# A delta-rule stage rewoven: one inversion on GpSimd, q projected ahead of z, weight loads from ScalarE's queue

## The chip, the cores and the metric

The kernel runs on one core of a Trainium2 chip. A core has five engines with queues of their own: TensorE (matrix products, called PE in the profile, with its weight loads as PEld), VectorE (DVE), ScalarE (ACT), GpSimd (POOL) and SyncE (SP), which here only orders transfers. The metric is the time on the device, in microseconds.

## The reference

Three token mixers and four feed-forward networks stand one after another on 256 tokens (272 with 16 meta tokens in the first part) of 1024 features, batch 1, in float32:

```python
h = concat(meta, x)
h = h + 0.5 * rmsnorm(swiglu(rmsnorm(h)))            # d_ff 2816
h = h + rmsnorm(mlstm_mixer(rmsnorm(h)))
h = h + 0.5 * rmsnorm(swiglu(rmsnorm(h)))
h = h[:, 16:]
h = h + gated_deltanet(rmsnorm(h))                   # the stage that is changed
h = h + conv_gated_mlp(rmsnorm(h))                   # its evictions carry the bias transfers
h = h + sliding_window_sink_attention(rmsnorm(h))    # uses a relative bias table
h = h + conv_gated_mlp(rmsnorm(h))
return rmsnorm(h)
```

The gated delta rule projects h to q and k (8 heads of 128), v and z (16 heads of 128) and two gates, runs a causal convolution of width 4 and a silu over q, k and v, normalizes q and k, and then, for each v head, with cumulated gates gc:

```python
decay = tril(exp(gc[:, None] - gc[None, :]))
m     = strict_tril((beta * k) @ k.T * decay)
t_mat = inverse(m + eye)                  # unit lower triangle
...                                       # u = t_mat @ (beta v), w = t_mat @ (beta k exp(gc))
o     = q_dec @ state + (q @ k.T * decay) @ v_new
o     = rmsnorm(o) * silu(z)
out   = o @ w_out
```

## The kernel before

Activations lie transposed in SBUF, features on partitions, tokens along the free axis. Weights come from HBM in halves of eight 128x128 tiles (512 KB, `load_half`): SyncE orders the transfer into one of four buffers `raw`, ScalarE casts it in two pieces to a high part `whi`, and VectorE subtracts to get the low part `wlo`. Each weight tile is then used in three matmuls (`mm3`, L250 to L252): high x high, high x low, low x high. `wtile` asks for halves three ahead, and five pairs of high and low parts are kept. One output block of 128 rows over 1024 inputs is 8 tiles, 24 matmuls, one half of weights.

The delta-rule stage is written in the order that a small planner, `Weave`, gives. It has fillers (the projections of the blocks in `GD_ORDER`, then the output projection `op_all`) and chains of dependent steps. A chain's step yields its cost on TensorE, a latency and its cost on VectorE; the planner advances a clock by them, takes a chain's step when its time has come, and otherwise one weight tile of the filler. The costs (`pe=0.32, dve=0.14` for one tile, `INVERT_COST = 55.0`) are figures in the source; they set the order in which instructions are written, and the engines then wait for each other by semaphores. The compiler keeps the order of each engine's queue near to it.

The chains: `norms` and `gates2` make the gate sums gc; they go to DRAM (`gcd`) and come back as 16 rows spread over all partitions (`gload`). `stage1(q8)`, for each key head, makes k k^T and q k^T, the decays from those rows on ScalarE, and the products U, N21 and A on VectorE; U goes to DRAM (`ud`). `front(0)` runs `stage1` of heads 0 to 3, `front(1)` of 4 to 7. `invert(hf)` loads the 64 diagonal blocks of 32x32 of one half into `B` (one block on each partition), and inverts them on GpSimd in 31 steps of two instructions (L1006 and L1011) on 64 partitions, copies (L1012) and stores to `xyd`. `levels(q8)` loads a head's U and its inverted blocks (`XY`, four transfers), joins the blocks to 128x128 in two levels with small matmuls (L1046 to L1076), and goes on with `solve` and `outp`, which ends with the parts that the output projection reads. `op_all` takes a head's parts as soon as its mark "h" stands. So `levels(0)` to `levels(3)` wait for `invert(0)` and `levels(4)` to `levels(7)` for `invert(1)`.

`outp` normalizes with `rsqrt_dve`, 14 small VectorE instructions, and scales with four ScalarE instructions from PSUM. `tanh_silu` and `zp` use tanh on ScalarE.

In the feed-forward network behind, `background` holds small jobs that are run one at every second eviction; among them eight transfers of 256 KB on GpSimd's queue that spread the bias table (`bias_tile`, L1215), each followed by an empty job.

Of the kernel before, what the change touches and what calls it, by code (L numbers as in the profile page):

```python
# [22 lines left out]
SEQ = 256  # L23
# [15 lines left out]
INVERT_COST = 55.0  # L39
GD_ORDER = [(kind, m) for kind, a, b in (("k", 0, 8), ("q", 0, 4), ("z", 0, 8), ("q", 4, 8), ("z", 8, 16), ("v", 0, 16))  # L40
# [80 lines left out]
def stack_kernel(ctx, tc, w, xt, cols, rows, gw, baw, rel, kc, kb, out):  # L121
# [31 lines left out]
    whole = {}  # L153

# [3 lines left out]
    def load_half(u, raw=None):  # L158
        if raw is None:
            raw = whole.get(u)  # L160
            if raw is None:
                raw = wraw.tile([128, 1024], F32, name="raw", tag="raw")
            lastw[0] = nc.sync.dma_start(out=raw, in_=w[u // 2, :, (u % 2) * 1024:(u % 2) * 1024 + 1024])
# [8 lines left out]
        for c in ((0, 512), (512, 1024)) if u == 0 else ((0, 1024),):  # L172
            V.tensor_tensor(out=lo[:, c[0]:c[1]], in0=raw[:, c[0]:c[1]], in1=hi[:, c[0]:c[1]].bitcast(F32),  # L173
                            op=ALU.subtract)
# [520 lines left out]
    ud = [gdr.tile([16, UG], F32, name=f"ud{i}") for i in range(2)]  # L695
    gcd = gdr.tile([16, 256], F32, name="gcd")
    xyd = [gdr.tile([64, 32, 64], F32, name=f"xyd{i}") for i in range(2)]
# [19 lines left out]
    with tc.tile_pool(name="gd", bufs=1) as gp, tc.tile_pool(name="gw", bufs=2) as gq:  # L717
        def unit():
            return gp.tile([128, SEQ], F32, name="u1k", tag="u1k", bufs=55)

        def unit_r():
            return gp.tile([128, SEQ], F32R, name="u1k", tag="u1k", bufs=55)
# [21 lines left out]
        fill = Weave(pe=0.32, dve=0.14)  # L744
# [15 lines left out]
        def ev_qk(m, ps):  # L760
            y = conv4((m + 8) % 16, ps, m >= 4)
            dst = unit()
            (kT if m < 8 else qT)[m % 8] = dst
            tanh_silu(dst, y)
            t = fill.work(1.2 if m >= 4 else 1.55)
            fill.free.append(t)
            fill.later(sumsq(m, dst), fill.work(0.34, t + 0.6 - fill.now) + 0.3)
# [21 lines left out]
        def vp(m):  # L789
# [9 lines left out]
            t = fill.work(1.2)  # L799
            fill.free.append(t)  # L800
            fill.later(vt(m, y), fill.work(0.34, t + 0.6 - fill.now) + 0.3)
# [71 lines left out]
        gct = gp.tile([16, SEQ], F32, name="gct")  # L873
        gcb = {}

        def gload(vh):
            if vh < 16:
                gcb[vh] = unit()
                nc.sync.dma_start(out=gcb[vh], in_=bass.AP(tensor=gcd.tensor, offset=gcd.offset + 256 * vh,
                                                           ap=[[0, 128], [1, 256]]))  # L880

        def gates2():
# [18 lines left out]
            yield 0.0, 1.5, 3.6  # L901
# [7 lines left out]
            pgt = ps_ax()  # L909
            for i in range(2):  # L910
                T_.transpose(pgt[:16, i * 128:i * 128 + 128], gc[:, i, :], ident)
            S.copy(gct, pgt[:16, 0:256])
            nc.sync.dma_start(out=gcd, in_=gct)
            yield 0.43, 2.5, 0.0
            gload(0)
            gload(1)
            gload(2)
            yield 0.0, 2.5, 0.0
# [4 lines left out]
        def urows(g):  # L923
            t = ud[g // 16]
            return bass.AP(tensor=t.tensor, offset=t.offset + (g % 16) * UG, ap=[[128, 128], [UG, 2], [1, 128]])

        def zp(m):
# [11 lines left out]
            fill.free.append(fill.work(0.34, 0.7))  # L939
            fill.mark("z", m)  # L940

        def stage1(q8):
# [10 lines left out]
            U, A[q8], N21[q8] = [unit(), unit()], [unit(), unit(), unit()], unit()  # L953
            for j in range(2):
                vh = 2 * q8 + j
                pg = gcb.pop(vh)
# [16 lines left out]
                V.tensor_tensor(out=A[q8][j].rearrange("p (a b) -> p a b", a=2), in0=pqm, in1=dv, op=ALU.mult)  # L973
                gload(vh + 3)
                fill.work(1.9)
                yield 0.64, 0.3, 0.0

        def front(hf):
            for q8 in range(4 * hf, 4 * hf + 4):
                while ("q", 8 + q8) not in fill.done:  # L980
                    yield 0.0, 0.5, 0.0
                yield from stage1(q8)
            fill.mark("s", hf)
# [7 lines left out]
        lastinv = [None]  # L991
        xyt = [gp.tile([128, 4, 256], F32, name=f"XY{i}") for i in range(3)]
        for t in xyt:
            P_.memset(t, 0.0)

        def invert(hf):
            p0 = 64 * hf
            pr = slice(p0, p0 + 64)
            X, Y = Z[pr, :, :, 0], Z[pr, :, :, 1]
            nc.sync.dma_start(out=B[pr], in_=bass.AP(tensor=ud[hf].tensor, offset=ud[hf].offset,  # L1000
                                                     ap=[[129 * 32, 64], [128, 32], [1, 32]]))
            first = None
            for i in range(31):
                n = 31 - i
                t = tmp[pr, 0:n * (i + 1)].rearrange("p (r j) -> p r j", r=n)
                ins = P_.tensor_tensor(out=t, in0=X[:, i, 0:i + 1].unsqueeze(1).to_broadcast([64, n, i + 1]),  # L1006
                                 in1=B[pr, i, i + 1:32].unsqueeze(2).to_broadcast([64, n, i + 1]), op=ALU.mult)
                if first is None and lastinv[0] is not None:
                    after(lastinv[0], ins)
                first = ins  # L1010
                P_.tensor_tensor(out=X[:, i + 1:32, 0:i + 1], in0=X[:, i + 1:32, 0:i + 1], in1=t, op=ALU.add)  # L1011
            lastinv[0] = P_.tensor_copy(Y, X.rearrange("p i j -> p j i"))  # L1012
            nc.gpsimd.dma_start(out=xyd[hf], in_=Z[pr].rearrange("p a b t -> p a (b t)"))
            fill.pool = max(fill.pool, fill.dve + 3.0) + INVERT_COST
            yield 0.0, fill.pool + 4.0 - fill.now, 0.0
            fill.mark("i", hf)

        def levels(q8):
# [3 lines left out]
            if q8 < 6:  # L1022
                XY = xyt[q8 % 3]
            elif q8 == 6:
                XY = gp.tile([128, 4, 256], F32, name="XY", tag="B")
                P_.memset(XY, 0.0)
            else:
                XY = gp.tile([128, 2048], F32, name="XY", tag="Z")[:, 0:1024].rearrange("p (g c) -> p g c", g=4)
                P_.memset(XY, 0.0)
            src = xyd[q8 // 4]  # L1030
            for a in range(4):
                ins = nc.sync.dma_start(out=XY[32 * a:32 * a + 32, :, 64 * a:64 * a + 64], in_=bass.AP(
                    tensor=src.tensor, offset=src.offset + (16 * (q8 % 4) + a) * 2048,
                    ap=[[64, 32], [4 * 2048, 4], [1, 64]]))
                after(lastw[0], ins)
            xyv = XY.rearrange("p g (c t) -> p g c t", t=2)
            X, Y = xyv[:, :, :, 0], xyv[:, :, :, 1]
            yield 0.0, 3.0, 0.0
# [5 lines left out]
            for b in (0, 64):  # L1044
                for g in range(4):
                    ins = T_.matmul(pr[b + 32:b + 64, g * 32:g * 32 + 32], us(g, b, 32, b + 32, 32), X[b:b + 32, g, b:b + 32],  # L1046
                                    start=True, stop=True)
                    if b == 0 and g == 0:
                        after(lastmm[0], ins)
# [15 lines left out]
            yield 1.0, 0.4, 0.8  # L1065
# [11 lines left out]
            yield 0.43, 0.4, 0.3  # L1077
            yield from solve(q8, Y)

        def solve(q8, Y):  # L1080
# [18 lines left out]
            yield 0.43, 0.4, 0.34  # L1099
            pw3 = ps_mm("mm")  # L1100
            for j in range(2):
# [3 lines left out]
                             scale=cc[:, 1, vh:vh + 1])  # L1105
            yield 0.43, 1.0, 0.0
            yield from outp(q8, pc)

        def outp(q8, pc):
# [15 lines left out]
            V.scalar_tensor_tensor(out=rv.rearrange("p (j i) -> p j i", j=2),  # L1125
# [330 lines left out]
```

## Time and profile before

| what | value |
|---|---|
| median of 3 runs | 1335.73 us (1334.15, 1335.73, 1347.11) |
| profiled execution | 1347.61 us |
| its span, first to last instruction | 1345.2 us |
| mean granted TensorE clock | 0.974 |
| TensorE busy | 97% of the span |
| VectorE, ScalarE, GpSimd busy | 70%, 59%, 8% |
| HBM read | 209.09 MB, 159 GB/s over the span |

The span is that of the instructions; the execution's own time has 2.4 us around it. A busy TensorE is one that has a matmul in its pipeline, whatever its clock; the granted clock is the share of full speed, 1.0 being 2.4 GHz and 0.5 being 1.2 GHz. The delta-rule stage runs from about 550 to 865 us of the span.

### The profile page before, as it was taken

Reading aid. Unit: us, or ns where it says so; the run is one execution under the profiler, and the core shown is the slowest. Engines: PE = TensorE matmul, PEld = TensorE weight load, DVE = VectorE, ACT = ScalarE, POOL = GpSimd, SP = SyncE. Lnnn points to the kernel's source line nnn. Section 1 sums busy time; section 2 is a strip of 40 time slices with the busy share of each in tenths; the row PEclk is TensorE's granted clock in tenths of the full one; section 3 lists DMA queues with packets and bytes.
Section 4 is the critical chain, followed back from the end, with each engine's and each line's share of the span. In section 5 each row is a group of like instructions: output and inputs, shape, how many; then the busy total and the mean of one; then the engine's idle time right before and its main releaser. Section 6 shows DMA issues by size and latency. Waiting matters only on the chain.

```text
span 1345.2 us, 27310 instructions
## 1 busy us (share of the span) xinstructions
PE 1304.8 (97%) x10635; PEld 1263.6 (94%) x10635; DVE 937.2 (70%) x1858; ACT 787.5 (59%) x1822; POOL 107.8 (8%) x163
## 2 busy tenths in 40 slices
PE   8999999999999999999898999999899999999997
PEld 8999999987999999999897899999899989999997
DVE  7866546775687764487894756887896686898852
ACT  6544445654665554466653746766665576777640
POOL 0000000000000000100598300001000000000000
PEclk9999999998999999999896998999999999999999
DMA  7755543541375555226554352468766432476540
GB/s 255 243 176 176 173 157 127 158 142 47 111 246 184 186 186 172 82 96 191 166 174 134 106 158 80 157 165 210 219 195 228 158 111 72 150 235 196 186 168 32
DMA packets 77761, 215.47 MB, mean 160 GB/s; under 512 B 16245, under 2 KB 27045, under 8 KB 77504
## 3 DMA queue, kind: packets, MB, share of 16 engines
q1 hardware_dynamic: 76224, 209.36, 48.8%
q0 software_dynamic: 1120, 3.85, 1.8%
q8 instruction: 84, 1.38, 0.4%
q10 hardware_dynamic: 288, 0.52, 0.1%
q14 instruction: 45, 0.37, 0.1%
HBM read 209.09 MB, written 4.60 MB: 159 GB/s over the span
## 4 chain that ended last, share of the span: by engine, by line
PE 78%; DMA 5%; DVE 5%; POOL 4%; ACT 4%; issue 2%; SPq 0%; DVEq 0%; ACTq 0%; POOLq 0%
PE mm L250 12%; PE mm L252 12%; PE mm L251 12%; PE st L250 7%; PE st L251 7%; PE st L252 7%; DMA raw<-in_w 4%; POOL tmp L1006 2%; PE mm L268 2%; POOL Z L1011 2%; PE mm L270 2%; PE mm L272 2%; DVE wlo L173 1%; ACT whi L171 1%; PE st L268 1%
## 5 line engine op out<-in xcount | busy, mean ns | idle before, releaser
L171 ACT CAST whi<-raw 128x512 fp32r<-128x512 f32 x752 | 438.1, 616 | 342.8 <-PE mm L251 118.9
L173 DVE TENSOR_TENSOR wlo<-raw,whi 128x1024 fp32r<-128x1024 f32 (+1 forms) x377 | 461.7, 1226 | 153.0 <-ACT whi L171 145.3
L252 PE MATMUL mm<-xh,wlo 128*128 128x256 f32 (+1 forms) x1040 | 295.4, 284 | 2.7 <-DVE wlo L173 2.7
L250 PE MATMUL mm<-xh,whi 128*128 128x256 f32 (+1 forms) x1040 | 295.7, 285 | 1.9 <-DVE fu L439 1.9
L251 PE MATMUL mm<-xl,whi 128*128 128x256 f32 (+1 forms) x1040 | 294.9, 284 | 0.0
L250 PE MATMUL st<-xh,whi 128*128 128x256 f32 (+1 forms) x720 | 208.3, 289 | 1.9 <-DVE fu L439 1.9
L251 PE MATMUL st<-xl,whi 128*128 128x256 f32 (+1 forms) x720 | 206.9, 287 | 0.0
L252 PE MATMUL st<-xh,wlo 128*128 128x256 f32 (+1 forms) x720 | 206.5, 287 | 0.1
L252 PEld LDWEIGHTS mm<-xh,wlo 128*128 128x128 f32 x1040 | 196.7, 189 | 3.2 <-DVE wlo L173 3.1
L250 PEld LDWEIGHTS mm<-xh,whi 128*128 128x128 f32 x1040 | 196.7, 189 | 2.3 <-ACT fu L436 2.1
L251 PEld LDWEIGHTS mm<-xl,whi 128*128 128x128 f32 x1040 | 196.4, 189 | 0.7 <-DVE xl L380 0.6
L250 PEld LDWEIGHTS st<-xh,whi 128*128 128x128 f32 x720 | 138.6, 192 | 3.2 <-ACT whi L171 2.0
L252 PEld LDWEIGHTS st<-xh,wlo 128*128 128x128 f32 x720 | 138.4, 192 | 0.4 <-DVE wlo L173 0.3
L251 PEld LDWEIGHTS st<-xl,whi 128*128 128x128 f32 x720 | 138.4, 192 | 0.1
L250 PE MATMUL mm<-hh,whi 128*128 128x256 f32 (+1 forms) x352 | 99.6, 283 | 0.0
L251 PE MATMUL mm<-hl,whi 128*128 128x256 f32 (+1 forms) x352 | 99.6, 283 | 0.0
L252 PE MATMUL mm<-hh,wlo 128*128 128x256 f32 (+1 forms) x352 | 99.6, 283 | 0.0
L250 PEld LDWEIGHTS mm<-hh,whi 128*128 128x128 f32 x352 | 67.0, 190 | 0.0
L251 PEld LDWEIGHTS mm<-hl,whi 128*128 128x128 f32 x352 | 66.5, 189 | 0.0
L252 PEld LDWEIGHTS mm<-hh,wlo 128*128 128x128 f32 x352 | 66.5, 189 | 0.0
L439 DVE SCALAR_TENSOR_TENSOR fu<-mm,colt,fu 128x255 f32<-128x255 f32 x108 | 51.2, 478 | 12.6 <-ACT fu L436 12.5
L1006 POOL TENSOR_TENSOR tmp<-Z,B 64x31 f32<-64x31 f32 (+15 forms) x62 | 43.9, 709 | 91.8 <-DMA B<-ud 87.1
(488 smaller groups left out, 2697.2 us busy)
## 6 DMA issues: line engine op xcount, KB each, us to landing
raw<-in_w SPq DMA_DIRECT2D x377, 512.0 KB, 4.0
u1k<-gcd SPq DMA_DIRECT2D x16, 128.0 KB, 3.5
ud<-u1k SPq DMA_DIRECT2D x16, 128.0 KB, 2.9
u1k<-ud SPq DMA_DIRECT2D x16, 128.0 KB, 2.5
Tb<-bvd POOLq DMA_DIRECT2D x8, 256.0 KB, 7.6
gx<-in_w SPq DMA_DIRECT2D x2, 512.0 KB, 6.9
xyd<-Z POOLq DMA_DIRECT2D x2, 512.0 KB, 5.2
XY<-xyd SPq DMA_DIRECT2D x32, 32.0 KB, 1.9
```

The costliest lines, as they stand in the source:

```text
L171: S.copy(hi[:, c[0]:c[1]], raw[:, c[0]:c[1]])
L173: V.tensor_tensor(out=lo[:, c[0]:c[1]], in0=raw[:, c[0]:c[1]], in1=hi[:, c[0]:c[1]].bitcast(F32), op=ALU.subtract)
L250: T_.matmul(ps, hi, xhh, start=first, stop=False)
L251: T_.matmul(ps, hi, xll, start=False, stop=False)
L252: lastmm[0] = T_.matmul(ps, lo, xhh, start=False, stop=last)
L268: T_.matmul(pss[j], wts[j][0], xhh, start=(k == 0), stop=False)
L270: T_.matmul(pss[j], wts[j][1], xhh, start=False, stop=False)
L272: T_.matmul(pss[j], wts[j][0], xll, start=False, stop=(k == kt - 1))
L439: V.scalar_tensor_tensor(out=t[:, d:], in0=ps[:, :T - d], scalar=wc(2 - d), in1=t[:, d:], op0=ALU.mult, op1=ALU.add)
L1006: ins = P_.tensor_tensor(out=t, in0=X[:, i, 0:i + 1].unsqueeze(1).to_broadcast([64, n, i + 1]), in1=B[pr, i, i + 1:32].unsqueeze(2).to_bro ...
L1011: P_.tensor_tensor(out=X[:, i + 1:32, 0:i + 1], in0=X[:, i + 1:32, 0:i + 1], in1=t, op=ALU.add)
```

## The change

The two halves of `front` and `invert` become one: `stage1` of all eight heads in a row, then one inversion on 128 partitions, and all `levels` wait for it; `levels(3)` and later also wait for `solve` of three heads earlier (mark "y"), and `XY` takes three tiles in turn, two of which lie where `Z` was. `B` is loaded in two transfers, one after each four heads. In `GD_ORDER` all of q comes before z. The gate sums no longer go through DRAM: TensorE transposes a broadcast column into PSUM for each head (`pgs`), and ScalarE reads that. While the fillers run, weight transfers are ordered on ScalarE's queue (`wq`), and outside of the planned time of the inversion every second half's low part is made on GpSimd (`share`); one of the products A moves to GpSimd too. In `outp` roots on ScalarE and a reciprocal replace `rsqrt_dve`, and two VectorE products replace the four scalings. The planner's costs change, and `fill.sp` spaces the loads of `levels`. The 8 bias transfers become 16 of half the size, one for every job.

```diff
-INVERT_COST = 55.0
-GD_ORDER = [... (("k", 0, 8), ("q", 0, 4), ("z", 0, 8), ("q", 4, 8), ("z", 8, 16), ("v", 0, 16))
+INVERT_COST = 54.0
+GD_ORDER = [... (("k", 0, 8), ("q", 0, 8), ("z", 0, 16), ("v", 0, 16))
...
+    wq, share = [nc.sync], [False]
-            lastw[0] = nc.sync.dma_start(out=raw, in_=w[...])
+            lastw[0] = wq[0].dma_start(out=raw, in_=w[...])
-            V.tensor_tensor(out=lo[...], in0=raw[...], in1=hi[...], op=ALU.subtract)
+            (P_ if share[0] and u % 2 else V).tensor_tensor(out=lo[...], in0=raw[...], in1=hi[...], op=ALU.subtract)
...
-        fill = Weave(pe=0.32, dve=0.14)
+        fill = Weave(pe=0.355, dve=0.08)
...
-            pgt = ps_ax()                      # gates2: gc to DRAM and back
-            S.copy(gct, pgt[:16, 0:256])
-            nc.sync.dma_start(out=gcd, in_=gct)
-            gload(0); gload(1); gload(2)
...
+            pgs = ps_mm("mm")                  # stage1
             for j in range(2):
-                pg = gcb.pop(vh)
+                pg = pgs[:, j * 256:j * 256 + 256]
+                for i in range(2):
+                    T_.transpose(pg[:, i * 128:i * 128 + 128], gc[:, i, vh:vh + 1].to_broadcast([128, 128]), ident)
...
-                V.tensor_tensor(out=A[q8][j]..., in0=pqm, in1=dv, op=ALU.mult)
-                gload(vh + 3)
-                fill.work(1.9)
-                yield 0.64, 0.3, 0.0
+                P_.tensor_tensor(out=A[q8][j]..., in0=pqm, in1=dv, op=ALU.mult)
+                t = fill.work(1.46)
+                yield 0.86, max(0.3, t - fill.now - 2.4), 0.0
...
-        def front(hf):
-            for q8 in range(4 * hf, 4 * hf + 4):
+        def front():
+            for q8 in range(8):
                 ...
+                if q8 % 4 == 3:
+                    pr = slice(16 * q8 - 48, 16 * q8 + 16)
+                    nc.sync.dma_start(out=B[pr], in_=bass.AP(tensor=ud.tensor, ...))
...
+        def invert():
+            share[0] = False
+            fill.fill_dve = 0.16
             for i in range(31):
-                ins = P_.tensor_tensor(out=t, in0=X[...].to_broadcast([64, n, i + 1]), ...)
+                P_.tensor_tensor(out=t, in0=X[...].to_broadcast([128, n, i + 1]), ...)
                 P_.tensor_tensor(out=X[...], in0=X[...], in1=t, op=ALU.add)
+            P_.tensor_copy(Y, X.rearrange("p i j -> p j i"))
+            for hf in range(2):
+                nc.gpsimd.dma_start(out=xyd[pr], in_=Z[pr]...)
+            fill.pool = max(fill.now, fill.dve) + 9.0 + INVERT_COST
+            yield 0.0, fill.pool + 3.0 - fill.now, 0.0
+            share[0] = True
...
-            ro = rsqrt_dve(rv, 4, sm)          # outp
-            for g in range(4):
-                S.activation(out=ob[g], in_=po[...], func=AF.Copy, scale=ro[:, g:g + 1])
+            for i in range(2):
+                S.activation(out=rvv[:, :, i], in_=ssv[:, :, i], func=AF.Sqrt, scale=4.0 / 128.0,
+                             bias=nq2[:, i, q8:q8 + 1])
+            V.reciprocal(rv, rv)
+            for j in range(2):
+                V.tensor_tensor(out=obs[j]..., in0=po[...], in1=rv[...].to_broadcast([128, 2, 128]), op=ALU.mult)
...
+        wq[0], share[0] = nc.scalar, True
-                       ([("g",)], front(0)), ([("s", 0)], invert(0)), ([("s", 0)], front(1)),
-                       ([("s", 1), ("i", 0)], invert(1))]
+                       ([("g",)], front()), ([("s",)], invert())]
         for q8 in range(8):
-            cond = [("i", q8 // 4)]
-            if 3 <= q8 < 6:
-                cond.append(("h", q8 - 3))
+            cond = [("i",)]
+            if q8 >= 3:
+                cond.append(("y", q8 - 3))
...
-    for a in range(8):
-        background += [lambda a=a: bias_tile(a), lambda: None]
+    for a in range(16):
+        background += [lambda a=a: bias_tile(a)]
```

## Rows read from the trace of the kernel before

**Rows 1.** The page, part 1: TensorE's busy time, share, instructions.
```profile
PE 1304.8 (97%) x10635; PEld 1263.6 (94%) x10635; DVE 937.2 (70%) x1858; ACT 787.5 (59%) x1822; POOL 107.8 (8%) x163
```

**Rows 2.** Windows: length, busy time and instructions by engine, granted clock, DMA share, GB/s.
```profile
450.00:500.00 50.00, 50.00 (x426) 50.00 (x425) 32.73 (x46) 25.15 (x50) 0.00 (x0) 1.00 0.59 186
...
575.00:865.00 290.00, 272.79 (x2332) 259.29 (x2331) 207.75 (x542) 175.81 (x496) 94.70 (x133) 0.91 0.45 138
...
625.00:655.00 30.00, 24.05 (x158) 23.18 (x157) 22.34 (x61) 22.21 (x62) 4.17 (x9) 0.83 0.67 192
...
715.00:755.00 40.00, 34.65 (x286) 31.36 (x286) 19.19 (x53) 18.37 (x59) 33.86 (x49) 0.66 0.46 143
755.00:795.00 40.00, 38.60 (x344) 36.43 (x345) 31.98 (x91) 29.14 (x90) 0.95 (x1) 1.00 0.39 113
795.00:825.00 30.00, 30.00 (x341) 27.15 (x340) 10.43 (x25) 11.42 (x37) 0.00 (x0) 0.77 0.36 121
...
885.00:905.00 20.00, 17.34 (x145) 16.93 (x144) 16.22 (x30) 11.40 (x25) 1.28 (x3) 1.00 0.72 179
...
940.00:960.00 20.00, 16.24 (x136) 15.89 (x136) 15.62 (x27) 11.74 (x26) 0.18 (x1) 1.00 0.86 230
```

**Rows 3.** Timeline of SyncE's queue, 685 to 760 us: start, length, what.
```profile
693.20 0.94 SPq L1021 DMA_DIRECT2D u1k<-ud  x2
710.24 1.76 SPq L1032 DMA_DIRECT2D XY<-xyd  x4
...
717.95 22.92 SPq L163 DMA_DIRECT2D raw<-in_w  x7
```

**Rows 4.** Timeline of ScalarE, 710 to 735 us.
```profile
722.03 1.14 ACT L171 CAST whi<-raw 128x512 fp32r<-128x512 f32 x2 [8.94 <-DMA raw<-in_w]
```

**Rows 5.** The chain of waits, 600 to 870 us: start, length, what.
```profile
616.61 2.48 DMA gcd<-gct
619.11 6.61 DMA u1k<-gcd
...
643.18 3.13 DMA ud<-u1k
646.47 3.60 DMA B<-ud
651.61 1.39 POOL tmp L1006
...
702.52 2.03 POOL Z L1012
```

**Rows 6.** Source line L1363, output transfers on ScalarE's queue: shortest, median, longest ns.
```profile
L1363 ACTq DMA_DIRECT2D out_t<-o x2: 338/357/376, 1340.4 to 1342.0; - x2
```

**Rows 7.** Timeline of all engines, 700 to 760 us, VectorE and GpSimd side by side.
```profile
700.75 1.30 DVE L173 TENSOR_TENSOR wlo<-raw,whi 128x1024 fp32r<-128x1024 f32 x1
...
701.04 1.09 POOL L1006 TENSOR_TENSOR tmp<-Z,B 64x31 f32<-64x31 f32 x1
...
702.22 0.24 POOL L1011 TENSOR_TENSOR Z<-Z,tmp 64x31 f32<-64x31 f32 x1
...
702.52 2.02 POOL L1012 COPY Z<-Z 64x1024 f32<-64x1024 f32 x1
...
703.22 1.61 DVE L758 SCALAR_TENSOR_TENSOR gy<-vs,gy 128x256 f32<-128x256 f32 x1
```

**Rows 8.** Timeline of GpSimd, 677 to 694 us.
```profile
685.69 0.69 POOL L1011 TENSOR_TENSOR Z<-Z,tmp 64x231 f32<-64x231 f32 x1
```

**Rows 9.** Groups by line, 560 to 900 us: busy us, mean ns; idle before.
```profile
L1131 ACT ACTIVATE u1k<-mm,rq_y 128x128 f32<-128x128 f32 x32 | 9.2, 376 | 2.1 <-DVE rq_y L292 2.1
...
L290 DVE TENSOR_TENSOR rq_t<-rq_t,rq_y 128x4 f32<-128x4 f32 (+1 forms) x27 | 4.3, 162 | 0.4
```

**Rows 10.** The page, part 6, DMA issues: KB each, median us to landing.
```profile
Tb<-bvd POOLq DMA_DIRECT2D x8, 256.0 KB, 7.6
```

**Rows 11.** Tile `raw`, 880 to 960 us: its transfers, shortest, median, longest.
```profile
DMA to landing us min/median/max: 3.5/5.9/9.3
```

More of the change, by code (lines that the diff above doesn't have):

```diff
@@ L694, in stack_kernel @@
     UG = 4 * 129 * 32
-    ud = [gdr.tile([16, UG], F32, name=f"ud{i}") for i in range(2)]
-    gcd = gdr.tile([16, 256], F32, name="gcd")
-    xyd = [gdr.tile([64, 32, 64], F32, name=f"xyd{i}") for i in range(2)]
+    ud = gdr.tile([32, UG], F32, name="ud")
+    xyd = gdr.tile([128, 32, 64], F32, name="xyd")
     n3 = []
@@ L764, in ev_qk @@
             tanh_silu(dst, y)
-            t = fill.work(1.2 if m >= 4 else 1.55)
+            t = fill.work(1.43 if m >= 4 else 1.85)
             fill.free.append(t)
-            fill.later(sumsq(m, dst), fill.work(0.34, t + 0.6 - fill.now) + 0.3)
+            fill.later(sumsq(m, dst), fill.work(0.47, t + 0.6 - fill.now) + 0.3)
         def sumsq(m, src):
@@ L798, in vp @@
             tanh_silu(y, y)
-            t = fill.work(1.2)
+            t = fill.work(1.43)
             fill.free.append(t)
-            fill.later(vt(m, y), fill.work(0.34, t + 0.6 - fill.now) + 0.3)
+            fill.later(vt(m, y), fill.work(0.47, t + 0.6 - fill.now) + 0.3)
         def vt(m, y):
@@ L989, in stack_kernel @@
         tmp = gp.tile([128, 256], F32, name="tmp")
[L991 to L1002, printed above, removed]
+        xyt = []
@@ L1018, in levels @@
+            yield 0.0, fill.pool + 3.0 - fill.now, 0.0
+            fill.mark("i")
+            share[0] = True
+            fill.fill_dve = 0.08
+            fill.sp = fill.now
         def levels(q8):
@@ L1021, in levels @@
                 nc.sync.dma_start(out=u[j], in_=urows(4 * q8 + 2 * j))
[L1022 to L1030, printed above, removed]
+            XY = xyt[q8 % 3]
             for a in range(4):
-                ins = nc.sync.dma_start(out=XY[32 * a:32 * a + 32, :, 64 * a:64 * a + 64], in_=bass.AP(
-                    tensor=src.tensor, offset=src.offset + (16 * (q8 % 4) + a) * 2048,
+                nc.sync.dma_start(out=XY[32 * a:32 * a + 32, :, 64 * a:64 * a + 64], in_=bass.AP(
+                    tensor=xyd.tensor, offset=xyd.offset + (16 * q8 + a) * 2048,
                     ap=[[64, 32], [4 * 2048, 4], [1, 64]]))
-                after(lastw[0], ins)
+            fill.sp = max(fill.sp, fill.now) + 2.8
             xyv = XY.rearrange("p g (c t) -> p g c t", t=2)
             X, Y = xyv[:, :, :, 0], xyv[:, :, :, 1]
-            yield 0.0, 3.0, 0.0
+            yield 0.0, fill.sp + 2.0 - fill.now, 0.0
             def us(g, r0, nr, c0, ncl):
@@ L1045, in levels @@
                 for g in range(4):
[L1046 to L1049, printed above, removed]
+                    T_.matmul(pr[b + 32:b + 64, g * 32:g * 32 + 32], us(g, b, 32, b + 32, 32), X[b:b + 32, g, b:b + 32],
+                              start=True, stop=True)
             for b in (32, 96):
```

89 lines of the change are left out of this document (39 added, 50 removed).

## The prediction

> **What bounds the kernel now.** I began with the page: TensorE is busy 97% of the span [rows 1], so a gain can only come from stretches in which it idles or is clocked down. The view of windows finds them: 50 us of plain feed-forward hold 426 matmuls, 0.117 us each, so a filler block of 24 weight matmuls takes 2.8 us; in a stretch the loss is its length less busy time times granted clock [rows 2]. The delta-rule stage (575 to 865 us) loses 290 - 272.8 x 0.91, about 40 us; its parts: 10.0 us at 625 to 655 (first half of `stage1`; 30 - 24.05 x 0.83), 17.1 at 715 to 755 (40 - 34.65 x 0.66) and 6.9 at 795 to 825 [rows 2]. The feed-forward part behind it loses 2.7 us at 885 to 905 and 3.8 at 940 to 960, where the bias transfers run [rows 2]. These 46 us are all the change can win; the rest of the page is TensorE at its pace.
>
> The SyncE timeline explains the largest loss: after the weight loads that end at 693.20 come two `u1k<-ud` loads of `levels(0)` and then four `XY<-xyd`, which start only at 710.24, when the first inversion has stored its result; the next weight load stands behind them and goes at 717.95 [rows 3]. So no weights were ordered for 25 us. ScalarE's next cast starts at 722.03 after 8.94 us of waiting for `raw` [rows 4], TensorE runs dry, and its granted clock is 0.66 in that stretch [rows 2], that is, part of it at 1.2 instead of 2.4 GHz, after an idle stretch.
>
> The chain of waits gives the second: the cumulated gates go through DRAM, 2.48 + 6.61 us [rows 5], then four key heads of `stage1` take from 625.7 to 643.2, then 3.13 us store and 3.60 us load, then GpSimd inverts from 651.6 to 702.5 [rows 5], and the second half of the heads starts after that. So `levels(4)` to `levels(7)` have their data some 40 us after the first four.
>
> **The change, part by part.** *Weight loads on ScalarE's queue.* They no longer stand behind `XY<-xyd`, and the 25 us hole goes. Each issue costs ScalarE 0.357 us, as the output's two there do [rows 6]; about 60 in the stage are 21 us, and ScalarE is busy 175.8 of 290 us [rows 2], so they fit into its idle time and cost the path nothing while the queue doesn't wait. What is new: a load waits for its `raw` buffer, that is, for the low part of four halves earlier, and behind it on ScalarE stand casts, PSUM copies and `stage1`'s exponentials. At no wait the cost is 0; at 1 us for each load it is 60 us of ScalarE. I take 1 us of path in all, since a load is needed only when four halves (11 us) are used up.
>
> A sentence of the Trainium skill speaks against this part: by "Trainium Kernel Development and Optimization", section Key Constraints, transfers issued from several engines' queues share the same DMA engines, and this saves only the issue time. The trace disagrees here, for the queue's order cost 25 us [rows 3] and issue time is a third of a microsecond [rows 6]; by that sentence the part would win next to nothing, which is the second rival below.
>
> *One inversion on 128 partitions, q ahead of z, gates transposed on TensorE.* Gone are the 9.1 us through DRAM [rows 5]. `stage1` of all eight heads runs in one go: at the rate of rows 5 (17.5 us for four) 35 us, from about 616 to 651; with 6.7 us store and load, inversion from 658. Its 62 steps on 128 partitions I take at the same 51 us as 64 partitions took [rows 5]; the bounds are that and twice that, since no row has such a step on 128 partitions. So `xyd` is written at 709 and all eight heads' data are there at about 716 instead of four at 710 and four at 757. Until then TensorE has the 32 blocks of z and v, 90 us, plus 14 us of `stage1` by the planner's 0.86 a head: 104 for the 100 us from 616. The cover just suffices, with 4 us over, some 10 with what is lost on the way. Then three heads' chains run (a chain is 5.7 us of TensorE by the planner's own figures, 17 for three) while the output projection waits for the first of them, some 25 to 30 us: about 12 us lost, partly at the lower clock, as at 795 to 825 now [rows 2]. So 17.1 + 6.9 becomes 12 to 13: **11 us won** (bounds 0 and 20).
>
> *stage1 itself.* Now the planner spaces its steps by VectorE's backlog and no gate load is awaited: of 10.0 us [rows 2] I leave 2.5. The added 32 transposes at 0.117 us each (the matmul pace of rows 2) are 3.8. **4 us won** (bounds -3 and 7). A third tile of the four `mm` banks for each head can hold up the next head's products; that is in the lower bound.
>
> *Half the low parts on GpSimd.* VectorE took 1.30 us for one [rows 7]. GpSimd's add of 231 elements took 0.69 us [rows 8] and of 31 elements 0.24 [rows 7]; the slope, 2.25 ns an element, gives about 2.5 us for 1024 (my value; bounds 1.3 as VectorE and 5). About 20 of them relieve VectorE of 26 us. But the two engines exclude each other: a 31-element product on GpSimd lasted 1.09 us beside a low part on VectorE, and VectorE's `gy<-vs,gy` lasted 1.61 us beside GpSimd's copy [rows 7]. So of the 26 us about half comes back as waits. None of it is on TensorE's path unless a low part is later than the 11 us for which its halves are cast ahead: 0 (bounds -4 and 3).
>
> The Trainium skill's "SBUF — State Buffer", section Who interferes with whom, says that a VectorE instruction with two inputs in SBUF and a GpSimd instruction that reads SBUF fully block each other; the trace agrees (1.61 us for 256 elements, where the low part takes 1.30 for 1024 [rows 7]). By that rule every GpSimd low part can hold up each such VectorE instruction for up to its 2.5 us, and the relief would be nil, which my zero already allows.
>
> *Roots on ScalarE in `outp`.* Away go 14 VectorE steps of 0.16 us, the four scalings on ScalarE at 0.376 us [rows 9]; in come two roots, a reciprocal and two VectorE products. Some 2 us less in each chain, and only the last counts at the end: **1 us** (bounds -3, if table loads between tanh and root fall among the v blocks, and 3).
>
> *Bias in 16 transfers.* The 256 KB transfers take 7.6 us to land [rows 10], and beside them weight loads take a median of 5.9 and up to 9.3 us, against 3.5 at best [rows 11]. Halved and spread one a step, the burst is half as long: of 6.5 us **3 won** (bounds 0 and 6.5).
>
> **Sum.** 11 + 4 + 1 + 3 - 1 = 18 us of the profiled execution, 1347.6 us (its span is 1345.2). The three timed runs have a median of 1335.7; the profiled one and one other stand 12 us higher. What lies in these 12 us no row says; if it is the lowered clock, the median has less to win. 34.65 x 0.34 is 11.8 us in 715 to 755 alone [rows 2]. So 10 to 18 us come off the median; I take 17, since the dry queue is in every run: **1319 us**.
>
> **Rivals.** *Nearly everything goes (1300).* Chains and fillers overlap as now at 755 to 795, where 40 us lose 1.4 [rows 2], and the lost 46 us shrink to 10. For it: the planner's figure for three matmuls becomes 0.355, which fits 3 x 0.117 [rows 2]. Against: the cover after 716 is thin.
>
> *The hole only moves (1331).* ScalarE's queue, in order, now holds casts behind loads that wait for low parts, or its exponentials and casts fill it in `stage1`; the 11 us shrink to 1 or 2, and 1335.7 - 5 remains. For it: ScalarE is already busy 22.2 of 30 us at 625 to 655 and gets a load more per block [rows 2].
>
> *The inversion comes too late (1360), slower.* There is one inversion and no head's chain before it; if a step on 128 partitions takes up to twice as long, or waits for VectorE's two-input instructions, data come at up to 767 instead of 716. TensorE then has about 10 us of blocks in reserve and stands still for the rest: 1335.7 - 17 + 51 - 10 = 1360. It decides from 27 us of lateness on (17 won and 10 in reserve); low parts queued behind the steps on GpSimd would add to it. For it: a step of 31 elements lasted 1.09 us beside a low part, where one alone took 0.24 [rows 7]. Against: the same happened in the 51 us that I use.
>
> The Trainium skill's "GPSIMD Engine Reference", section 2 (Architecture), says that each of eight cores serves its own 16 partitions and all get every instruction; by that 128 partitions take no longer than 64. No run here shows it yet; it speaks against this rival.
>
> **How the numbers follow.** Forecast 0.49, nearly everything 0.11, the hole moves 0.24, too late 0.16 (whole or half). A difference of 1% is 13 us, about the spread of the three runs, and what can be told from no change. The forecast's own width (10 to 20 us off) puts a tenth of it within 1%; so faster by over 1%: 0.44 + 0.11 = 0.55. Within 1%: 0.05 + 0.22 = 0.27. Slower by over 1%: 0.16 and 0.02 of the moved hole, 0.18. The range reaches from the better rival, 1299, to a lateness of 37 us, 1345; outside stay a part of the first and the doubled inversion.
>
> **What would show it.** After: no gap of over 10 us between weight loads; one inversion of about 51 us from about 658; all L1046-like matmuls after 716 and in threes; in 625 to 655 a clock of 1.0; a loss of some 12 us behind 716; raw loads under 7 us beside the bias. Wrong if casts wait for loads held on ScalarE, if GpSimd's steps are longer on 128 partitions, or if the v blocks end before 710.

## The result and the profile after

The changed kernel takes **1360.59 us** (median, 1355.42 to 1363.15), the kernel before 1335.74 in the same comparison: ratio **1.0156**, 95% interval 1.012 to 1.0193 (the two medians alone give 1.0186; the four times of the kernel before go from 1334.15 to 1347.11). It is slower by 1.6%, not faster by 1.2%. The profiled execution has a span of 1361.4 us and a time of 1363.15.

Page of the changed kernel, part 1 (answers [rows 1]), and the bias transfers of part 6 (KB each, median us to landing; [rows 10]):

```profile
PE 1298.9 (95%) x10665; PEld 1259.9 (93%) x10665; DVE 914.1 (67%) x1727; ACT 780.0 (57%) x1805; POOL 129.0 (9%) x149
...
Tb<-bvd POOLq DMA_DIRECT2D x16, 128.0 KB, 5.9
```

TensorE idles for 1361.4 - 1298.9 = 62.5 us, before for 1345.2 - 1304.8 = 40.4 [rows 1]. The windows of the changed kernel say where (columns as in [rows 2]):

```profile
585.00:685.00 100.00, 96.11 (x752) 93.13 (x752) 69.31 (x189) 61.01 (x162) 41.32 (x40) 0.97 0.50 152
625.00:655.00 30.00, 29.44 (x230) 28.24 (x229) 16.27 (x53) 20.45 (x60) 15.17 (x13) 1.00 0.55 154
685.00:825.00 140.00, 101.45 (x942) 95.15 (x941) 69.80 (x131) 63.63 (x181) 47.49 (x57) 0.79 0.36 110
705.00:735.00 30.00, 1.26 (x11) 1.05 (x9) 0.36 (x1) 0.54 (x3) 19.53 (x34) 0.56 0.20 44
905.00:1000.00 95.00, 95.00 (x811) 94.98 (x810) 81.65 (x140) 64.24 (x137) 13.90 (x28) 1.00 0.79 211
```

For 30 us from 705, TensorE, VectorE and ScalarE all do next to nothing; only GpSimd works. By the prediction's measure (length less busy time times granted clock) 685 to 825 loses 140 - 101.45 x 0.79 = 59.9 us. The same stretch of the kernel before, which holds the 17.1 and 6.9 us of [rows 2]:

```profile
585.00:685.00 100.00, 93.28 (x725) 91.07 (x725) 83.06 (x217) 64.52 (x168) 31.66 (x41) 0.95 0.56 170
685.00:825.00 140.00, 130.51 (x1203) 120.96 (x1202) 85.78 (x207) 76.57 (x227) 61.49 (x90) 0.85 0.43 130
825.00:905.00 80.00, 76.34 (x635) 73.92 (x634) 67.81 (x175) 58.70 (x151) 3.42 (x7) 1.00 0.48 139
905.00:1000.00 95.00, 91.09 (x767) 90.53 (x766) 76.85 (x128) 60.69 (x129) 4.61 (x13) 1.00 0.74 214
```

That is 29.1 us lost before, so 31 us came in, while `stage1` (585 to 685) loses 6.8 instead of 11.4 and the stretch beside the bias 0 instead of 3.9. (How far such losses differ between two executions of the same instructions is shown at d_bias16: by some 5 us in 685 to 825.)

Who stopped first? The view of waits of the changed kernel, 695 to 745 us (us in all, times, longest):

```profile
ACT Vn L810 <- DMA XZ<-xyd: 31.9, 1, 31.9
DVE gy L758 <- ACT vs L757: 30.1, 1, 30.1
...
PE ax L808 <- DVE gy L758: 29.6, 1, 29.6
```

Read from below: TensorE waits for VectorE, VectorE for ScalarE, ScalarE for a load of `XZ`. But line 810, a copy of a v head, reads no `XZ`. The timeline of ScalarE shows what stands ahead of it (answers [rows 4]; ACTq rows are its DMA issues):

```profile
702.09 0.47 ACT L737 ACTIVATE gy<-st,colt 128x256 f32<-128x256 f32 x1
734.08 0.34 ACTq L164 DMA_DIRECT2D raw<-in_w  x1
734.46 0.37 ACT L810 ACTIVATE Vn<-ax,nkh 128x128 f32<-128x128 f32 x1 [31.90 <-DMA XZ<-xyd]
```

What stands ahead of the copy is a weight load. SyncE's timeline in the same time (answers [rows 3]):

```profile
672.93 11.50 SPq L1009 DMA_DIRECT2D u1k<-ud  x6
728.24 2.91 SPq L1012 DMA_DIRECT2D XYB<-xyd  x4
731.97 3.63 SPq L1012 DMA_DIRECT2D XZ<-xyd  x8
```

SyncE waits for the inverse until 728.24, as before until 710.24. The weight loads have left its queue, and still one of them goes out only at 734.08. The order of the compiled program, with the semaphores each instruction waits for, tells why. It is the program's listing and no view of the profile (`[waits ...]`; the first number counts an engine's instructions):

```
SyncE    204 L1012 DMA XYB<-xyd [waits DMAHW5,DMASW3,Pool]
         205 to 207 XYB<-xyd    [waits DMAHW6] [DMAHW7] [DMAHW0]
         208 L1012 DMA XZ<-xyd  [waits DMAHW2,DMASW4,Pool]
         209 L1012 DMA XZ<-xyd  [waits DMAHW3]
         210 to 215 XZ<-xyd     [waits DMAHW5] [6] [7,Pool] [0] [1] [2]
ScalarE  873 L164 DMA raw<-in_w [waits DMAHW1]   (its cast: waits DMAHW1)
         876 L164 DMA raw<-in_w                  (its cast: waits DMAHW4)
         887 L737 ACTIVATE gy<-st,colt
         888 L164 DMA raw<-in_w [waits DMAHW3]   (its cast: waits DMAHW3)
         889 L810 ACTIVATE Vn<-ax,nkh
```

The transfers of the two queues take turns at eight completion semaphores, 0 to 7, in the order of the program: XYB has 5, 6, 7, 0, a weight load 1, XZ 2 and 3, a weight load 4, XZ 5, 6, 7, 0, 1, 2, and then the weight load at place 888 is again at 3. Before it may use 3, the second XZ transfer, on the other queue, must have landed. That one belongs to the row at 731.97, the second of its eight issues; the chain of waits has it at 732.32 with 1.74 us, so it has landed at 734.06, and the weight load goes at 734.08. The chain of the changed kernel, 600 to 745 us (answers [rows 5]):

```profile
662.05 3.60 DMA ud<-u1k
665.76 7.15 DMA B<-ud
673.04 0.88 POOL tmp L986
...
721.83 1.87 POOL Z L989
724.57 6.32 DMA xyd<-Z
731.00 0.96 POOL XZ L997
732.32 1.74 DMA XZ<-xyd
734.08 3.89 DMA raw<-in_w
```

The inversion began 15 us late and took about what was predicted: its steps run from 673.04 to 721.83, 48.8 us (51 predicted), with the copy behind them to 723.70. From 705.35 on VectorE stood still beside them; what the steps take beside a busy VectorE is told below.

Two things of the whole diff, left out of the lines printed ahead of the prediction, had no step in it: the kernel before held the first chain matmul (L1046) behind the last filler matmul and the `XY` loads behind the last weight load, each with an `after(...)`; the change drops both.

### The profile page after: what moved, and what is told of

The parts are those of the page before. It is cut to its first block, busy times and chain, and to the rows that moved or that the text cites. A ratio compares the mean times of both kernels' runs of the same rounds, so it can differ in the third digit from the quotient of the medians.

```text
span 1361.4 us, 27159 instructions
## 1 busy us (share of the span) xinstructions
PE 1298.9 (95%) x10665; PEld 1259.9 (93%) x10665; DVE 914.1 (67%) x1727; ACT 780.0 (57%) x1805; POOL 129.0 (9%) x149
## 4 chain that ended last, share of the span: by engine, by line
PE 84%; DMA 4%; POOL 4%; DVE 3%; ACT 3%; issue 2%; SPq 0%; ACTq 0%; DVEq 0%; POOLq 0%
PE mm L251 13%; PE mm L253 12%; PE mm L252 12%; PE st L251 7%; PE st L252 7%; PE st L253 7%; DMA raw<-in_w 3%; PE mm L269 2%; PE mm L271 2%; PE mm L273 2%; POOL Z L988 2%; POOL tmp L986 2%; PE st L269 1%; PE st L273 1%; PE st L271 1%
## 5 line engine op out<-in xcount | busy, mean ns | idle before, releaser
L174 DVE TENSOR_TENSOR wlo<-raw,whi 128x1024 fp32r<-128x1024 f32 (+1 forms) x358 | 438.0, 1225 | 156.2 <-ACT whi L172 145.2
L251 PE MATMUL mm<-xh,whi 128*128 128x256 f32 (+1 forms) x1072 | 305.4, 285 | 1.3 <-ACT xh L380 1.3
L253 PE MATMUL mm<-xh,wlo 128*128 128x256 f32 (+1 forms) x1072 | 304.6, 284 | 0.0
L252 PE MATMUL mm<-xl,whi 128*128 128x256 f32 (+1 forms) x1072 | 304.2, 284 | 0.1
L251 PEld LDWEIGHTS mm<-xh,whi 128*128 128x128 f32 x1072 | 202.8, 189 | 3.1 <-ACT xh L380 2.2
L251 PE MATMUL st<-xh,whi 128*128 128x256 f32 (+1 forms) x704 | 202.1, 287 | 1.5 <-DVE gy L739 1.3
L252 PEld LDWEIGHTS mm<-xl,whi 128*128 128x128 f32 x1072 | 202.5, 189 | 0.5 <-DVE xl L381 0.5
L253 PEld LDWEIGHTS mm<-xh,wlo 128*128 128x128 f32 x1072 | 202.7, 189 | 0.1
L252 PE MATMUL st<-xl,whi 128*128 128x256 f32 (+1 forms) x704 | 201.0, 286 | 0.0
L174 POOL TENSOR_TENSOR wlo<-raw,whi 128x1024 fp32r<-128x1024 f32 x19 | 45.3, 2384 | 500.4 <-ACT whi L172 434.2
```

The source lines that it names most:

```text
L174: (P_ if share[0] and u % 2 else V).tensor_tensor(out=lo[:, c[0]:c[1]], in0=raw[:, c[0]:c[1]], in1=hi[:, c[0]:c[1]].bitcast(F32), op=ALU.s ...
L251: T_.matmul(ps, hi, xhh, start=first, stop=False)
L252: T_.matmul(ps, hi, xll, start=False, stop=False)
L253: lastmm[0] = T_.matmul(ps, lo, xhh, start=False, stop=last)
```

## The experiments

Ratios are to the kernel before on the same chip, whose median there was 1340 to 1341 us (1335.74 in the comparison above), so differences of medians between two versions can be off by a few us. The first six move the queues and the orders about.

**Weights back on SyncE's queue** (a_sp), all else of the change kept.

```
-        wq[0], share[0] = nc.scalar, True
+        share[0] = True
```

> The changed kernel with one part undone: weight loads stay on SyncE's queue. Theory (a weight load on ScalarE's queue waits for a transfer of inverted blocks on SyncE, 702 to 734 us, and holds up all of ScalarE): the 32 us stop of ScalarE goes; a hole without weight loads may come back on SyncE behind the XY loads, as before (25 us). 1330 to 1350 us. Rival (TensorE would stand still anyhow, since the one inversion ends at 724 and nothing else is left to do): TensorE idle for 25 us before 735 as now, 1355 to 1365 us.

1358.13 us, ratio 1.0141 (1.0098 to 1.0185). The stop is as long, in the queue where it was before. SyncE's timeline of this run:

```profile
687.76 4.25 SPq L164 DMA_DIRECT2D raw<-in_w  x2
725.90 1.55 SPq L1012 DMA_DIRECT2D XYB<-xyd  x2
727.56 0.61 SPq L164 DMA_DIRECT2D raw<-in_w  x1
```

Weight loads stand behind `XYB` from 692 to 727. So ScalarE's queue is not needed for the stop; weight loads that wait for XY loads, on either queue, are enough. The edit moved something else as well. A v block leaves two transposes on TensorE (L808), and 24 of the 32 start before the first chain matmul (L1026, at 756.0): 12 of the 16 v blocks stand ahead of it. In the changed kernel it is 12 before 740.8, so 6 blocks. The order on TensorE followed the weights' queue, though no line of it was edited.

**XY loads on GpSimd's queue** (a_xyp), weights on ScalarE's as in the change.

```
-                nc.sync.dma_start(out=XY[32 * a:32 * a + 32, ...], in_=bass.AP(
+                nc.gpsimd.dma_start(out=XY[32 * a:32 * a + 32, ...], in_=bass.AP(
```

> The changed kernel, with the loads XY<-xyd ordered on GpSimd's queue instead of SyncE's, so that no transfer that waits for the inversion stands on a hardware queue; weight loads stay on ScalarE's. Theory (shared wait between the two hardware queues): no stop of ScalarE at 702 to 734, the v blocks go on until the inversion ends, 1328 to 1340 us. Rival (one inversion too late, fillers gone): TensorE idles for 25 us before 735 all the same, 1355 to 1365. A third: GpSimd, waiting for XY tiles to come free, holds up its low parts, and some of the gain is lost again after 740.

1354.69 us, 1.0123 (1.0086 to 1.016). ScalarE's stop at a load is gone, but TensorE stops all the same. Its waits, 700 to 745 us:

```profile
ACT Vn L810 <- PE ax L808: 24.6, 3, 20.6
...
PE mm L1026 <- issue: 23.6, 1, 23.6
```

Now L1026, the first chain matmul, stands at the head of TensorE's queue for 24 us, and the v blocks behind it can't pass. Only 6 of the 16 v blocks come ahead of it, as in the changed kernel. That is a second cause under the first.

**Both** (a_spxyp): weights on SyncE's, XY on GpSimd's queue.

> Both at once: weight loads on SyncE, XY<-xyd on GpSimd. Nothing that waits for the inversion stands before a weight load in any queue. Theory: fastest of the three, 1318 to 1335 us, at or below the kernel before. Rival (ScalarE's queue was the gain and the inversion the loss): as a_xyp or slower, above 1350.

1336.96 us, 0.9986 (0.9959 to 1.0013). 1.7% of the time is back, and SyncE orders 16 weight loads in a row from 686.18 to 752.35. 12 v blocks stand ahead of L1026, as in a_sp.

**Only ScalarE's queue** (b_actq): the kernel before with its weight loads of the stage there.

```
+        wq[0] = nc.scalar      # around the stage; the XY loads' after(lastw[0], ins) left out
```

> The kernel before with one part of the change alone: weight loads of the delta-rule stage on ScalarE's queue (the order against XY loads on SyncE's queue is left out there, since it has no meaning across queues). Theory: two inversions, so two times at which XY loads stand waiting on SyncE; a weight load on ScalarE's queue waits for one of them and stops ScalarE for 5 to 30 us each; 1340 to 1375. Rival (the queue is harmless; the loss is in the rest of the change): 1320 to 1335, since the 25 us hole on SyncE goes.

1395.37 us, 1.0423 (1.038 to 1.0466). Alone this edit costs 55 us: with two inversions there are two stops. Its waits, 670 to 775 us, show both instructions of ScalarE that wait for a transfer they don't read:

```profile
ACT Vn L811 <- DMA XY<-xyd: 30.6, 1, 30.6
...
ACT zt L936 <- DMA XY<-xyd: 25.4, 1, 25.4
```

**The queues mended the other way** (e_xyp_pin58): weights on ScalarE's queue, XY on GpSimd's, and TensorE's order held again.

```
-INVERT_COST = 54.0
+INVERT_COST = 58.0
+                    if b == 0 and g == 0:
+                        after(lastmm[0], ins)     # first L1026 behind the last filler matmul
```

> The changed kernel with its weight loads on ScalarE's queue as it has them, but the XY loads on GpSimd's queue, the first chain matmul held behind the last filler matmul again, and the planner's price of the inversion at 58 instead of 54 (so that some 11 v blocks, not 6, stand ahead of the first chain matmul on TensorE). Theory (ScalarE's queue cost time only because a weight load there waited for an XY load stuck on SyncE's, and TensorE's order cost the rest): with both gone the queue is harmless and the time is that of the version with weights on SyncE and XY on GpSimd, 1337 us, 1331 to 1342. Rival (a weight load on ScalarE's queue is dear in itself, by holding up casts behind it): 1350 or more.

1334.63 us, 0.9953 (0.9933 to 0.9972). It differs from a_xyp by TensorE's order (12 v blocks ahead of L1026 instead of 6) and the planner's price alone, and by 20 us; no run parts the order's line from the price. With no load in it that shares a semaphore with a stuck transfer, ScalarE's queue costs nothing that shows against SyncE's (1336.96 in a_spxyp).

**The two dropped orders alone** (e_sp_pin54): weights and XY on SyncE's queue, both `after` lines back.

```
+                after(lastw[0], ins)              # XY loads
+                        after(lastmm[0], ins)     # first L1026
```

> The changed kernel with weight loads and XY loads both on SyncE's queue and the two orders of the kernel before written back (XY loads behind the last weight load issued, first chain matmul behind the last filler matmul). Theory (what matters is how many v blocks' loads stand ahead of the first XY load): the orders alone do not put more loads ahead of it, so weight loads still stand behind the XY loads, a stretch without TensorE stays, and the time is 1345 to 1360. Rival (the two orders that were removed are the whole loss): 1330 to 1340.

1353.92 us, 1.0092 (1.0069 to 1.0116). Against a_sp, which has the same queues, the two lines bring 4 us. TensorE has 12 v blocks ahead of the first chain matmul, as it had in a_sp without them, so what they moved is SyncE's order: it now issues eight weight loads by 712.7 and then stands until 733.93 at `XYB`. TensorE's stop comes later and the time is lost all the same: 725 to 785 loses 60 - 40.25 x 0.66 = 33.4 us. A good order on TensorE is not enough.

The next four take parts of the mended version (a_spxyp, 1336.96) out again.

**No low parts on GpSimd** (c_noshare: `share[0] = True` dropped).

> The same version with every low part on VectorE. Theory of the prediction (relief and mutual waits cancel): within 4 us of 1337, if the order of the queues stays alike. Rival (GpSimd low parts are late behind XY loads and hold up TensorE): 5 to 12 us less. Second rival (the relief was worth it): 5 to 15 us more, with VectorE above 85% busy in 590 to 660.

1329.48 us, 0.992 (0.9894 to 0.9945): the low parts on GpSimd cost 7.5 us by the medians, and the two intervals don't overlap. Windows of this run:

```profile
585.00:685.00 100.00, 99.02 (x796) 95.75 (x795) 80.61 (x205) 65.54 (x172) 32.92 (x44) 1.00 0.64 181
685.00:825.00 140.00, 127.43 (x1242) 119.94 (x1241) 83.72 (x173) 80.95 (x256) 53.88 (x73) 0.89 0.39 112
```

585 to 685 loses 1.0 us, with the low parts on GpSimd (a_spxyp) 100 - 95.84 x 0.98 = 6.1, and the inversion starts at 662.0 instead of 668.0. Side by side in a_spxyp's timeline, VectorE and GpSimd:

```profile
595.83 0.17 DVE L290 TENSOR_TENSOR rq_t<-ssk,rq_y 128x16 f32<-128x16 f32 x1
...
597.36 2.09 DVE L290 TENSOR_TENSOR rq_t<-ssk,rq_y 128x16 f32<-128x16 f32 x1
...
597.01 2.41 POOL L174 TENSOR_TENSOR wlo<-raw,whi 128x1024 fp32r<-128x1024 f32 x1 [4.85 <-DVE rq_y L293]
```

A 16-element step of the roots, 0.17 us by itself, lasts 2.09 us while GpSimd takes a low part, until that ends (597.01 + 2.41 = 599.42; 597.36 + 2.09 = 599.45). Another such step (L860) lasts 2.07 us from 604.58, and one of 256 elements (L758) 1.78 us from 616.23, where 0.43 is common. The roots' small steps are a serial chain ahead of `stage1`: these three holds add some 5 us by estimate (1.9 + 1.9 + 1.35), near to the 6 by which the inversion starts later. By these rows what GpSimd takes over is dear by whom it stops; where the rest of the 7.5 us lies is not shown.

**A later inversion in the planner** (c_inv60: `INVERT_COST = 60.0`).

> The version with weight loads on SyncE and XY loads on GpSimd (1337 us), with INVERT_COST 60 instead of 54, so that two more v blocks (6.6 us with their transposes) stand before the first chain matmul in TensorE's queue. Theory (what is left of the stop, 727 to 734 us, is TensorE's own queue: the first small matmuls stand before v blocks that could run): 6 to 12 us less, 1325 to 1331, with no lowered clock behind it. Rival (the stop is only the end of available work, moved): within 3 us of 1337.

1331.6 us, 0.9932 (0.991 to 0.9955): 14 v blocks ahead of L1026 instead of 12, and 5 us.

**Bias in 8 transfers again** (c_bias8: the 8 transfers of 256 KB of the kernel before).

> The same version with the bias in 8 transfers of 256 KB again. Theory: the loss of 5 to 6 us in the feed-forward part behind the stage comes back, 1341 to 1344, and weight loads beside them take up to 9 us. Rival (the transfers were not the cause, the start of the feed-forward part is): within 2 us of 1337.

1350.6 us, 1.0072 (1.0047 to 1.0098): 13.6 us more. Window of this run:

```profile
905.00:1000.00 95.00, 89.74 (x743) 89.19 (x742) 75.33 (x123) 59.60 (x125) 4.53 (x9) 0.98 0.71 200
```

It loses 7.1 us there, a_spxyp 0.7; with 865 to 905 it is 9.7 against 1.6, so that the profiles show some 8 of the 13.6.

**Roots on VectorE again** (c_rsq: `rsqrt_dve` and the four scalings of the kernel before).

> The same version with the old normalization in outp, 14 small VectorE instructions and four scalings on ScalarE. Theory: 1 to 4 us more (1338 to 1341), since only the last chain's 2 us stand on the path. Rival (table loads between tanh and root cost more than they save): 0 to 4 us less.

1338.47 us, 0.9997 (0.9978 to 1.0016): 1.5 us, within the measurement.

The last two are the kernel before with one number or one part changed.

**The hole of the kernel before filled** (d_b70).

```
-INVERT_COST = 55.0
+INVERT_COST = 70.0
```

> The kernel before with only the planner's price of one inversion raised from 55 to 70, so that seven weight loads come between the second B load and the first XY load on SyncE's queue. Theory (the 25 us hole of the kernel before is weight loads waiting behind XY loads that wait for the second inversion): the hole shrinks by the work that those loads feed, some 10 to 17 us, 1319 to 1328 us. Rival (the hole has another cause, or the work is then missing later beside the chain): 1334 to 1345.

1340.74 us, 1.001 (0.9985 to 1.0035): nothing won, against my theory. Windows of this run, and under them the same of the kernel before:

```profile
685.00:725.00 40.00, 37.95 (x352) 36.34 (x351) 36.10 (x61) 29.23 (x72) 36.04 (x49) 1.00 0.72 210
725.00:785.00 60.00, 57.92 (x499) 52.31 (x498) 34.88 (x110) 33.44 (x111) 24.19 (x37) 0.86 0.40 111
785.00:825.00 40.00, 35.23 (x337) 31.86 (x337) 14.38 (x45) 13.95 (x50) 0.00 (x0) 0.66 0.24 71
```

```profile
685.00:725.00 40.00, 32.66 (x300) 30.69 (x299) 25.98 (x42) 20.52 (x49) 35.66 (x54) 0.91 0.58 171
725.00:785.00 60.00, 58.05 (x485) 53.71 (x485) 42.39 (x121) 37.94 (x121) 25.83 (x37) 0.83 0.34 105
785.00:825.00 40.00, 39.79 (x422) 36.55 (x422) 17.41 (x45) 18.10 (x59) 0.00 (x0) 0.83 0.41 126
```

The hole did shrink: 685 to 725 loses 2.1 us instead of 10.3. But 785 to 825 loses 40 - 35.23 x 0.66 = 16.7 instead of 7.0: the v blocks that filled the hole are missing beside the last chains. From 685 to 825 it is about 29 us in both.

**Only the bias in 16 transfers** (d_bias16).

> The kernel before with only the bias in 16 transfers. By the profiled stretches of the prediction: 3 us won, 1333 to 1338. By what taking the 16 transfers out of the repaired version cost (13 us by its medians, 8 by its profiles): 1322 to 1330. Rival (nothing in this kernel, the split only pays beside other parts of the change): 1339 to 1342.

1333.49 us, 0.9942 (0.9917 to 0.9967): 6.6 us, 4 to 11 by the interval. Windows of this run:

```profile
685.00:825.00 140.00, 128.79 (x1230) 118.84 (x1229) 90.19 (x248) 81.56 (x256) 54.61 (x84) 0.90 0.43 124
825.00:905.00 80.00, 76.29 (x612) 74.17 (x612) 67.14 (x144) 56.15 (x130) 4.69 (x12) 0.96 0.56 156
905.00:1000.00 95.00, 95.00 (x815) 95.00 (x814) 78.29 (x126) 63.29 (x131) 9.76 (x25) 1.00 0.84 221
```

905 to 1000 is filled, 95.00 of 95 busy at full clock, but 825 to 905 loses 6.8 us, before 3.7. So the times say that the split wins, and the profile doesn't say where. It says another thing: up to the bias this program has the instructions of the kernel before in the same order, and yet 685 to 825 loses 24.1 us here and 29.1 there (785 to 825 ran at a clock of 1.00, before 0.83). Two profiles of one program differ by some 5 us in this stretch, and a smaller difference between two versions' windows shows nothing.

## Why the prediction was wrong

**The step that failed** is "Weight loads on ScalarE's queue": 1 us of path, "since a load is needed only when four halves (11 us) are used up". The stop at 705 to 735 begins with that load: ScalarE stood 31.9 us for it. I had a queue that waits among the unknowns, but only for a `raw` buffer, and the low parts that free it. What the queue waited for was a semaphore that the program's transfers share, and through it the very XY loads from which the weights had been taken away. The trace shows the wait and the order of the program the turn-taking; that a XY load on GpSimd's queue takes ScalarE's stop away (a_xyp) bears it out, and two stops with two inversions (b_actq) too. The issues themselves cost what I said: 0.335 us, the median of the weight loads at 700 to 760 us, against 0.357. The Trainium skill's sentence that queues save only issue time ("Trainium Kernel Development and Optimization", section Key Constraints) does not fit: a_sp and a_spxyp differ by the XY loads' queue alone, with 12 v blocks ahead of L1026 in both, and took 1358.13 and 1336.96. Where no load stands behind a stuck one, the queue made no difference that shows (a_spxyp and e_xyp_pin58), as the sentence has it.

**What I overlooked** is TensorE's order. With 6 v blocks ahead of the first L1026, TensorE stops even when all loads are in time (a_xyp). The dropped order leaves the compiler free to do so; with the weight loads on SyncE's queue it put 12 ahead without being told (a_sp, a_spxyp). Neither cause alone is the loss: a_sp and e_sp_pin54 mend the order and not the loads, a_xyp the loads and not the order, and they win 2 to 7 us by their medians; a_spxyp and e_xyp_pin58 mend both and win 24 to 26.

**The worth of the hole** was mis-taken as well, and this holds for the mended kernel. I counted 17.1 us as to be won because TensorE is dry there. But the blocks that fill it are the same that run beside the chains later (d_b70: hole filled, time unchanged). The 24.0 us of the two stretches were to fall by 11; the whole of 685 to 825, which holds them, loses 26.6 in c_noshare (140 - 127.43 x 0.89), and 29.1 or 24.1 in two profiles of the old stage (before, d_bias16). My rival *the hole only moves* had this result, but put it down to casts behind loads. Of the 41.6 us between 1319 and 1360.6, both causes above are 24 to 26 and the low parts below 7.5; the some 10 that are left are near to the 11 counted for the hole.

**One inversion.** Right: 128 partitions cost what 64 do. Two of the shortest pairs of steps of 252 elements, in the changed kernel (L986, L988) and, under it, before (L1006, L1011):

```profile
704.62 0.62 POOL L986 TENSOR_TENSOR tmp<-Z,B 128x252 f32<-128x252 f32 x1
705.32 0.73 POOL L988 TENSOR_TENSOR Z<-Z,tmp 128x252 f32<-128x252 f32 x1
```

```profile
721.63 0.61 POOL L1006 TENSOR_TENSOR tmp<-Z,B 64x252 f32<-64x252 f32 x1
722.32 0.73 POOL L1011 TENSOR_TENSOR Z<-Z,tmp 64x252 f32<-64x252 f32 x1
```

The Trainium skill's "GPSIMD Engine Reference", section 2 (Architecture), by which all cores get every instruction, agrees with these numbers. But the total is no fixed price. Before, the 62 steps took 52.3 us in the first inversion (its first step stands at 650.21; the 651.6 of the prediction is only where the chain of waits joins it) and 43.5 in the second, 705.48 to 749.02; VectorE was busy for 47 us of the one and 20 of the other. In the mended version, where VectorE works on beside them (47 us), a_spxyp's timeline of GpSimd has them from 667.95 to 724.23, 56.3 us:

```profile
667.95 1.06 POOL L986 TENSOR_TENSOR tmp<-Z,B 128x31 f32<-128x31 f32 x1 [6.84 <-DMA B<-ud]
...
724.23 2.16 POOL L989 COPY Z<-Z 128x1024 f32<-128x1024 f32 x1
```

So the 48.8 us of the changed kernel, near to the predicted 51, may owe something to VectorE's stop; no run separates that. Wrong: the start, 673 instead of 658. `ud` and `B` took 3.60 + 7.15 us instead of 3.13 + 3.60 [rows 5], and `stage1` ended at 662 instead of 651. The rival *the inversion comes too late* named 1360 and the time was 1360, but its mechanism, data 27 us late or more by longer steps, did not happen: that the number fits is luck.

**`stage1`.** 4 us won predicted; 625 to 655 runs at a clock of 1.00, as forecast. 585 to 685 loses 4.6 less than before (11.4 to 6.8), of which some 2 can be the execution (d_bias16 loses 100 - 93.09 x 0.97 = 9.7), and without the low parts on GpSimd 10.4 less.

**Half the low parts on GpSimd.** The duration was right, the path was not: 2.386 us each (predicted 2.5), but 7.5 us lost, outside my bounds of -4 and 3. Tile `wlo` of the changed kernel, 560 to 900 us (ns, shortest, median, longest):

```profile
L174 DVE TENSOR_TENSOR wlo<-raw,whi x46: 1201/1224/1664, 581.6 to 898.5; 128x1024 fp32r<-128x1024 f32 x46
L174 POOL TENSOR_TENSOR wlo<-raw,whi x18: 2337/2386/2428, 578.4 to 871.7; 128x1024 fp32r<-128x1024 f32 x18
```

I priced the exclusion by VectorE's busy time, where a long instruction loses a part. It is priced by the chain it hits: a step of 0.17 us is held for 2.

**Roots** 1 us predicted, 1.5 by medians and not told from nothing; one table load at the roots (L1106, 1.28 us at 790.09). **Bias** 3 of at most 6.5 predicted; 6.6 alone, 13.6 taken out of the mended version. The term was mis-sized, and its reason is not shown: the weight loads beside it land hardly sooner (median 5.5 us and up to 8.2 in 880 to 960 of the changed kernel, before 5.9 and 9.3 [rows 11]), and 825 to 1000, which holds the two windows that I counted, loses 6.8 us in d_bias16 and 7.6 before. Why it is twice as much beside the other parts, no run separates.

The best version is the change with weights on SyncE's queue, XY loads on GpSimd's, and all low parts on VectorE: 1329.5 us, 0.8% under the kernel before. The bias alone brings most of that (0.9942, with the rest 0.992; the intervals overlap), so that merging the inversion, in the best order I ran, is not shown to win anything.

## What to carry to other kernels

Moving loads to another engine's queue frees them only if nothing that they share, completion semaphores too, can be held by the transfer they flee; read from the compiled order which earlier transfer each one waits for, and follow what stands behind it. A hole is worth filling only with work that is not needed as filler later: count the filler once for the whole stage, not for each hole. An edit that deletes an explicit order, or moves loads to another queue, can change the order of an engine that it doesn't name: read that order before pricing the edit. And before a few us of one profile's stretch are taken for a prize, see how much that stretch differs in another execution.

## What the runs showed of the hardware

A weight load on ScalarE's queue stood 31.9 us for a transfer on SyncE's queue that it has no data in common with, and held up every ScalarE instruction behind it. A VectorE step of 16 elements lasted 2.09 us instead of 0.17 beside a GpSimd low part of 2.41 us, and ended with it. An unhindered GpSimd step of 252 elements took 0.62 (product) or 0.73 us (sum) on 128 partitions and 0.61 or 0.73 on 64; the 62 steps together took 48.8 us (the changed kernel) to 56.3 (a_spxyp) on 128 partitions and 43.5 and 52.3 (before) on 64. The same instructions up to the bias, in two executions, lost 24.1 and 29.1 us of TensorE's time in the same 140 us, with 785 to 825 at a clock of 1.00 in one and 0.83 in the other.
